# A transformer layer on one core: the output projection as seven half-size products, with its weight sums, one modulation row and several loads made elsewhere

## The chip, the core and the metric

The kernel runs on one core of one Trainium2 chip. The metric is the device time of one execution in microseconds. Three runs of the kernel before took 1303.9, 1304.48 and 1306.3 us; the median is 1304.48 us.

## The reference

One layer on 512 tokens of width 1024, in float32. Three stages each add to x, and each normalises x and modulates it with three of nine rows (`sh`, `sc`, `g`) that are computed from a conditioning vector c:

```python
mod = jax.nn.silu(c) @ w_ada + b_ada          # nine rows of 1024
u = rms_norm(x, ffn1_norm_g) * (1 + sc1) + sh1
x = x + 0.5 * g1 * swiglu(u, ffn1_w_in, ffn1_w_out)
u = rms_norm(x, mix_norm_g) * (1 + sc2) + sh2
z = u @ w_mix + b_mix      # 4 mLSTM heads, 16 forgetting-attention heads, 2 gates
merged = sigmoid(g_a) * (y_a @ w_branch_a) + sigmoid(g_b) * (y_b @ w_branch_b)
x = x + g2 * (merged @ w_out)                 # 512x1024 times 1024x1024
u = rms_norm(x, ffn2_norm_g) * (1 + sc3) + sh3
x = x + 0.5 * g3 * swiglu(u, ffn2_w_in, ffn2_w_out)
```

## The kernel before

Every large product is made of triples of TensorE matmuls (`mm3`, L139): each float32 operand is split into a high part in a reduced format (`fp32r`) and the remainder, and hi·hi, hi·lo and lo·hi are summed in one PSUM bank (lines L141 to L143). ScalarE makes the high part of a weight tile (`wh`, L116) and VectorE subtracts it from the tile that was loaded (`wl`, L118). Loads go through SyncE's queue into a ring of three buffers called `raw` (L106). A `raw` buffer is free again when its `wl` is made.

The program runs through these stages: the first FFN's input product (`ffn_in`) up to about 279 us, its output product (`pair_out`) up to about 371 us, the mix norm, the gates, mLSTM and the attention heads up to about 817 us, the two branch products with the gating ("br", to 906.5 us), the product with `w_out` (to 953 us), and the second FFN. The three FFN and branch stages fill spare time of VectorE and the queues with side work that is stepped by generators: `ada_row(v)` (L305) adds up one row v of `w_ada` in eight steps, each a 512 KB load and a multiply-add on VectorE (L320), and `ada_sum` closes the row with two matmuls (L372).

In the branch stage, the two halves of a merged tile are added on GpSimd (L1691), split by ScalarE (L1692) and VectorE (L1693). The product with `w_out` has two halves of 512 columns. `token_gemm` makes half 0 into four PSUM banks (k outer, four token blocks inner), `residual` scales each finished bank with `g` and adds it to x (L796, L798), and `x_sq` (L243) sums the squares on ScalarE. `passage` makes half 1 in the same way and starts the second FFN in it: with `xnorm` (L256) and `norm_turn` (L286) it normalises and transposes tokens 0 to 255 as soon as both halves of them are done, and tokens 256 to 511 after the last block. Between these two, `first(0, ...)` runs the first products of the second FFN on tokens 0 to 255. Inside `passage` all instructions are pinned to the order in which they are written; elsewhere a scheduler orders them, and each engine then executes its list strictly in that order. A normalisation is: `v` (L261) from the sums, eight small VectorE operations (`rsqrt`, L151), two scalings on VectorE (L267) and two on ScalarE (L268), 16 transposes (L294), and per k tile a `u_part` (L272) of two ScalarE operations and one subtraction on VectorE.

In the heads, `fox_s` leaves exp'd scores S and their row sums `sm`. `fox_p` inverts the sums (L1323), scales S in four pieces (L1326, VectorE) and transposes it (L1332).

The functions that the diff touches follow.

Of the kernel before, what the change touches and what calls it, by code (L numbers as in the profile page):

```python
# [22 lines left out]
NT = 4  # L23
# [24 lines left out]
class Layer:  # L48
    def __init__(self, tc, es, A, out, dbg=None):
# [13 lines left out]
        self.due = []  # L63
        self.posts = []
# [191 lines left out]
    def xnorm(self, hf, pool):  # L256
# [5 lines left out]
        r = self.rsqrt(v, 2, self.pin, D ** 0.5)  # L262
# [410 lines left out]
    def token_gemm(self, lhs, nk, w, half, done, tail=2, extra=None):  # L673


        nch = nk // 2
        bank = self.tbank if half == 0 else self.gbank
        ps = [bank() for _ in range(NT)]
        def step(tb, ch, wc):
            for k2 in range(2):  # L680
                k = 2 * ch + k2
                lh, ll = lhs(k)
                self.mm3(ps[tb], lh[:, tb * P:(tb + 1) * P], ll[:, tb * P:(tb + 1) * P],
                         wc[0][:, k2, :], wc[1][:, k2, :], k == 0, k == nk - 1)
        for ch in range(nch - tail):
            wc = self.w_mov(w, ch * 256, half * 512)
            for tb in range(NT):
                step(tb, ch, wc)
            if extra:
                extra()  # L690
        wcs = [self.w_mov(w, ch * 256, half * 512) for ch in range(nch - tail, nch)]
        for tb in range(NT):
            for i, wc in enumerate(wcs):
                step(tb, nch - tail + i, wc)
            done(tb, half, ps[tb])

    def passage(self, lhs, w_out, w_in, bp, G, sh):

        nc, tc = self.nc, self.tc
        pin = tc.keep_in_program_order  # L700
        done = self.residual(0.5, 5, 1, bp)
        ps = [self.gbank() for _ in range(NT)]
        def step(tb, ch, wc, k2s=(0, 1)):
            for k2 in k2s:
                k = 2 * ch + k2
                lh, ll = lhs(k)
                self.mm3(ps[tb], lh[:, tb * P:(tb + 1) * P], ll[:, tb * P:(tb + 1) * P],
                         wc[0][:, k2, :], wc[1][:, k2, :], k == 0, k == NK - 1)
# [4 lines left out]
        def apart(m):  # L713
            r = load(m)
            half = lambda n: [bp.tile([P, 4, P], F32R, name=self.nm(n), tag="yl", bufs=8) for _ in range(2)]
            hi, lo = half("fh"), half("fl")
            for i in range(2):
                pin(nc.scalar.activation(hi[i], r[:, 4 * i:4 * i + 4], AF.Copy))
            ws[m] = lambda k: (hi[k // 4][:, k % 4, :], lo[k // 4][:, k % 4, :])
            def rest():  # L720
                for i in range(2):
                    pin(nc.vector.tensor_tensor(lo[i], r[:, 4 * i:4 * i + 4], hi[i], op=SUB))
            return rest
        def whole(m):
# [5 lines left out]
                    lambda: pin(nc.vector.tensor_tensor(lo, r, hi, op=SUB)))  # L730
        wc = self.w_mov(w_out, 0, 512)
        for tb in range(NT):
            step(tb, 0, wc)
        wcs = [self.w_mov(w_out, ch * 256, 512) for ch in range(1, 4)]
        self.pin = pin
        for f in whole(0):
            f()
# [23 lines left out]
        for k in range(1, 5):  # L761
            part(0, b, k, True)
# [998 lines left out]
```

## Time and profile before

| What | Value |
|---|---|
| Runs | 1303.9, 1304.48, 1306.3 us |
| Profiled execution: span | 1304.7 us (no time besides it is listed for this execution) |
| TensorE busy | 1291.3 us, 99% |
| VectorE busy | 961.2 us, 74% |
| ScalarE busy | 632.3 us, 48% |
| GpSimd busy | 34.6 us, 3% |
| Granted TensorE clock | 9 or more tenths in all 40 slices |
| DMA | 260.48 MB, 199 GB/s of HBM traffic over the span |

The shares are averages over stages with different limits. TensorE's busy time counts a matmul from its modelled start to its modelled end, and matmuls overlap, so the cost of one matmul is read from the distance between two starts. A wait shows where that distance is larger.

### The profile page before, as it was taken

Reading aid. Unit: us, or ns where it says so; the run is one execution under the profiler, and the core shown is the slowest. Engines: PE = TensorE matmul, PEld = TensorE weight load, DVE = VectorE, ACT = ScalarE, POOL = GpSimd, SP = SyncE. Lnnn points to the kernel's source line nnn. Section 1 sums busy time; section 2 is a strip of 40 time slices with the busy share of each in tenths; the row PEclk is TensorE's granted clock in tenths of the full one; section 3 lists DMA queues with packets and bytes.
Section 4 is the critical chain, followed back from the end, with each engine's and each line's share of the span. In section 5 each row is a group of like instructions: output and inputs, shape, how many; then the busy total and the mean of one; then the engine's idle time right before and its main releaser. Section 6 shows DMA issues by size and latency. Waiting matters only on the chain.

```text
span 1304.7 us, 17739 instructions
## 1 busy us (share of the span) xinstructions
PE 1291.3 (99%) x6265; PEld 1085.2 (83%) x6265; DVE 961.2 (74%) x1740; ACT 632.3 (48%) x1040; POOL 34.6 (3%) x57
## 2 busy tenths in 40 slices
PE   8999999999999999999999999999999999999998
PEld 6788888888889888788888888888898888888887
DVE  6877777478789787999998776677566656635787
ACT  5633232355467655666574766234372223223741
POOL 1000000000010101000000000003000000000000
PEclk9999999999999999999999999999999999999999
DMA  9999978464865534545455583777539778634573
GB/s 294 276 328 303 316 266 292 139 185 155 296 187 144 173 89 130 178 133 155 138 128 149 130 151 102 230 256 242 186 114 321 257 233 278 219 97 136 167 272 143
DMA packets 245257, 260.48 MB, mean 200 GB/s; under 512 B 57312, under 2 KB 184960, under 8 KB 245168
## 3 DMA queue, kind: packets, MB, share of 16 engines
q1 hardware_dynamic: 240464, 251.41, 63.0%
q10 hardware_dynamic: 4384, 7.88, 2.0%
q8 instruction: 49, 0.80, 0.3%
q14 instruction: 40, 0.33, 0.1%
q0 software_dynamic: 320, 0.06, 0.0%
HBM read 220.43 MB, written 38.87 MB: 199 GB/s over the span
## 4 chain that ended last, share of the span: by engine, by line
PE 93%; DVE 4%; DMA 1%; ACT 1%; issue 1%; POOL 0%; ACTq 0%; DVEq 0%; POOLq 0%; SPq 0%
PE g L142 24%; PE g L141 24%; PE g L143 24%; PE t L141 4%; PE t L142 4%; PE t L143 4%; PE g L949 2%; PE t L1362 1%; PE t L1332 1%; PE t L1305 1%; PE t L949 1%; PE t L1306 1%; PE t L837 0%; DVE wl L118 0%; DMA h_d<-hn 0%
## 5 line engine op out<-in xcount | busy, mean ns | idle before, releaser
L116 ACT ACTIVATE wh<-raw 128x1024 fp32r<-128x1024 f32 (+2 forms) x246 | 248.9, 1016 | 348.8 <-PE g L142 109.9
L118 DVE TENSOR_TENSOR wl<-raw,wh 128x1024 fp32r<-128x1024 f32 (+2 forms) x246 | 288.1, 1175 | 155.0 <-ACT wh L116 131.0
L141 PE MATMUL g<-uh,wh 128*128 128x512 f32 (+1 forms) x880 | 340.9, 387 | 0.0
L143 PE MATMUL g<-uh,wl 128*128 128x512 f32 (+1 forms) x880 | 339.6, 386 | 0.0
L142 PE MATMUL g<-ul,wh 128*128 128x512 f32 (+1 forms) x880 | 339.1, 385 | 0.0
L143 PEld LDWEIGHTS g<-uh,wl 128*128 128x128 f32 x880 | 165.3, 188 | 33.6
L141 PEld LDWEIGHTS g<-uh,wh 128*128 128x128 f32 x880 | 165.4, 188 | 32.9 <-issue 0.6
L142 PEld LDWEIGHTS g<-ul,wh 128*128 128x128 f32 x880 | 165.4, 188 | 32.2
L141 PE MATMUL g<-wh,uh 128*128 128x512 f32 (+1 forms) x256 | 97.6, 381 | 0.0
L143 PE MATMUL g<-wh,ul 128*128 128x512 f32 (+1 forms) x256 | 96.6, 377 | 0.0
L142 PE MATMUL g<-wl,uh 128*128 128x512 f32 (+1 forms) x256 | 96.5, 377 | 0.0
L320 DVE SCALAR_TENSOR_TENSOR acc<-raw,ccol,acc 128x1024 f32<-128x1024 f32 (+1 forms) x56 | 56.7, 1032 | 40.1 <-DMA raw<-in_w_ada_dram 40.0
L141 PE MATMUL t<-wh,A 128*128 128x512 f32 x176 | 68.6, 390 | 0.0
L142 PE MATMUL t<-wl,A 128*128 128x512 f32 x176 | 68.6, 390 | 0.0
L143 PEld LDWEIGHTS g<-wh,ul 128*128 128x128 f32 x256 | 48.2, 188 | 8.9
L142 PEld LDWEIGHTS g<-wl,uh 128*128 128x128 f32 x256 | 48.3, 188 | 8.4
L141 PEld LDWEIGHTS g<-wh,uh 128*128 128x128 f32 x256 | 48.2, 188 | 8.2
L141 PE MATMUL g<-yh,wh 128*128 128x512 f32 x128 | 49.8, 389 | 0.0
L143 PE MATMUL g<-yh,wl 128*128 128x512 f32 x128 | 49.8, 389 | 0.0
L142 PE MATMUL g<-yl,wh 128*128 128x512 f32 x128 | 49.8, 389 | 0.0
L1316 ACT ACTIVATE S<-S,mn 128x128 f32<-128x128 f32 (+1 forms) x64 | 35.6, 557 | 26.2 <-DVE mn L1308 20.4
L460 ACT ACTIVATE A<-E 128x768 fp32r<-128x768 f32 x22 | 18.6, 846 | 52.6 <-DVE E L459 52.6
(370 smaller groups left out, 2230.3 us busy)
## 6 DMA issues: line engine op xcount, KB each, us to landing
raw<-in_ffn_w_in_dram SPq DMA_DIRECT2D x82, 512.0 KB, 4.9
raw<-in_w_ada_dram SPq DMA_DIRECT2D x48, 512.0 KB, 4.8
raw<-in_w_mix_dram SPq DMA_DIRECT2D x46, 512.0 KB, 4.3
sa<-in_ffn_w_out_dram SPq DMA_DIRECT2D x22, 512.0 KB, 5.4
sb<-in_ffn_w_out_dram SPq DMA_DIRECT2D x44, 256.0 KB, 5.7
ws<-sa SPq DMA_DIRECT2D x22, 512.0 KB, 4.8
ws<-sb SPq DMA_DIRECT2D x44, 256.0 KB, 3.8
raw<-ws SPq DMA_DIRECT2D x44, 256.0 KB, 3.6
```

What stands on the lines that cost most here:

```text
L116: nc.scalar.activation(hi, src, AF.Copy)
L118: self.last_lo = nc.vector.tensor_tensor(lo, src, hi, op=SUB)
L141: pin(mm(ps, lh, rh, start=start, stop=False))
L142: pin(mm(ps, lh, rl, start=False, stop=False))
L143: self.last_mm = pin(mm(ps, ll, rh, start=False, stop=stop))
L320: nc.vector.scalar_tensor_tensor(a, r[:, s], c, a, op0=MUL, op1=ADD)
L460: nc.scalar.activation(A1[:, 0:3, :], E[:, 0:3, :], AF.Copy)
L949: pin(nc.tensor.matmul(acc_ps[b], (wl if p == 1 else wh)[:, b % 2, s], self.ul[k] if p == 2 else self.uh[k], start=k == 0 and p == 0, stop ...
L1305: nc.tensor.matmul(ps[:, :w], q[:, s], k[:, :w], start=True, stop=False)
L1306: nc.tensor.matmul(ps[:, :w], q[:, s], kl[:, :w], start=False, stop=True)
L1316: nc.scalar.activation(S[:, ws], S[:, ws], AF.Exp, scale=-1.0, bias=m, accum_out=sm[:, qb:qb + 1])
L1332: tr = lambda b, c, qb, kb: nc.tensor.transpose(b[:, c:c + P], S[:, P_OFF[qb] + kb * P:P_OFF[qb] + (kb + 1) * P], self.ident)
```

## The change

1. **The product with `w_out`** is made by a scheme of seven products of half size (256 tokens by 512 inner by 512 columns) in place of eight. Their names are A11, A12, S2, S1, S4, S3 and A22. Each has 4 k tiles, 2 token blocks and 3 matmuls of 128x512, so there are 168 matmuls in place of 192. Partial results are kept in `p1`, `u2` and `u4` and added again; S1 and S4 go on in the same two banks (`Z`) in which S2 was summed, after a copy of each (L771) was taken.
2. **Sums and differences of operands.** `merge_pair` forms those of the merged tiles on VectorE beside the branch products, and the GpSimd addition goes to VectorE. `out_sums` forms those of the weights beside heads 10 to 16: for each of four i, two loads of 256 KB and four stores on GpSimd's queue, and four additions of 128x512 on VectorE.
3. **The scaling of S** goes to ScalarE for heads 9 to 15.
4. **Modulation row 6** is added up in the first FFN's input stage (32 steps in place of 24) and not in the branches.
5. **Loads.** x, the row `g` and the rows 6 and 7 are loaded within the branches, and the 16x16 transpose of the rows (L389) goes there too. Two of the first weight tiles of the second FFN are loaded into free buffers (`fr`, four loads of 256 KB) and not through the `raw` ring.
6. **The passage** is written anew: the token blocks of x are finished in another order, all four sums of squares of tokens 256 to 511 stand behind the first `norm_turn` (before, two of them did), and `first(0, (0, 1, 2))` is one group ahead of the second `norm_turn`.

```diff
-                ada = (s for v in (3, 4, 2) for s in self.ada_row(v, new, row, self.gbank if v == 2 else self.tbank))
+                ada = (s for v in (3, 4, 2, 6) for s in self.ada_row(v, new, row, self.tbank if v < 6 and v > 2 else self.gbank))
-                    if n * 7 % 10 < 7:
+                    if n * 3 % 4 < 3 or n > 23:
                         next(ada, None)
-        self.ada = (s for v in (6, 7) for s in self.ada_row(v, new, row, self.gbank))
+        self.ada = self.ada_row(7, new, row, self.gbank)
...
-            nc.vector.tensor_scalar(S[:, ws], S[:, ws], sm[:, qb:qb + 1], None, op0=MUL)
+            if h < 9:
+                nc.vector.tensor_scalar(S[:, ws], S[:, ws], sm[:, qb:qb + 1], None, op0=MUL)
+            else:
+                nc.scalar.activation(S[:, ws], S[:, ws], AF.Copy, scale=sm[:, qb:qb + 1])
...
+    def out_sums(self, w, ip):
+        for i in range(NK // 2):
+            with self.tc.issue_after(self.last_raw.ins):
+                for r in range(2):
+                    nc.gpsimd.dma_start(t[:, 2 * r:2 * r + 2, :], w[(2 * i + r) * P:(2 * i + r + 1) * P, :]
+                                        .rearrange("p (h n) -> p h n", h=2))
+            yield
+            with self.tc.issue_after(self.last_lo.ins):
+                V(a, b, a, op=SUB)
+                V(b, d, b, op=SUB)
+            yield
+            with self.tc.issue_after(self.last_lo.ins):
+                V(d, d, a, op=SUB)
+                V(c, c, d, op=SUB)
+            yield
+            for n, o in enumerate(self.wo):
+                nc.gpsimd.dma_start(o[:, i, :], t[:, n, :])
+            yield
...
             for m in range(NK):
                 t = self.branch(m, 1, bp, None)
+                nc.vector.tensor_tensor(self.merge_slot(m, yp), t, ta[m], op=ADD)
                 step()
-                nc.gpsimd.tensor_tensor(t, t, ta[m], op=ADD)
-                nc.scalar.activation(self.mh[m], t, AF.Copy)
-                nc.vector.tensor_tensor(self.ml[m], t, self.mh[m], op=SUB)
...
+                if m % 2:
+                    self.merge_pair(m // 2, bp)
+                if 0 < m < 5:
+                    self.x_tiles((m - 1,))
+                    self.x_load(self.x_d, (m - 1,))
...
+        def product(n, ps, tb, start=False):
+            s = slice(tb * P, (tb + 1) * P)
+            for i in range(NK // 2):
+                h, l = self.ma[n][i]
+                w = self.ops[n][i // 2]
+                self.mm3(ps[tb], h[:, s], l[:, s], w[0][:, i % 2, :], w[1][:, i % 2, :], start and i == 0, i == NK // 2 - 1, True)
...
+        product("S2", Z, 0)
+        copy(u2[0], Z[0])
+        t = into(1, 0, X[1], p1[1])
+        product("S2", Z, 1)
+        copy(u2[1], Z[1])
+        fetch("S4")
...
+        product("S1", Z, 0)
...
         b = self.norm_turn(0, xn)
+        product("A22", V4, 1)
...
+        t20 = into(2, 0, V4[0])
+        part(0, 0)
+        part(0, 1)
+        lo3()
+        into(2, 1, ts[0])
+        part(0, 2)
+        part(0, 3)
+        into(3, 1, ts[1])
+        part(0, 4)
+        self.x_sq(2, 0, t20)
+        part(0, 5)
+        self.x_sq(2, 1, ts[0])
+        t = into(3, 0, V4[1])
+        part(0, 6)
+        self.x_sq(3, 1, ts[1])
+        part(0, 7)
+        self.x_sq(3, 0, t)
         xn = self.xnorm(1, bp)
```

Three places show how the instruction lists change. In the rows, a line number is that of the kernel named, then come the operation, the tile written, the tiles read and the shape.

**VectorE, the second norm of the passage.** Before (`v` from the sums, seven small operations, then the scaling `xn`):

```order
L261 SCALAR_TENSOR_TENSOR v_9338<-ss_8913 128x2
L160 TENSOR_SCALAR rq_9340<-v_9338 128x2
L162 TENSOR_TENSOR rt_9341<-rq_9340 128x2
L163 SCALAR_TENSOR_TENSOR rd_9343<-rt_9341,v_9338 128x2
L164 TENSOR_SCALAR rd_9343<-rd_9343 128x2
L165 SCALAR_TENSOR_TENSOR rt_9341<-rd_9343 128x2
L166 SCALAR_TENSOR_TENSOR rt_9342<-rd_9343 128x2
L167 SCALAR_TENSOR_TENSOR rq_9340<-rt_9341,rq_9340 128x2
L168 SCALAR_TENSOR_TENSOR rq_9340<-rt_9342,rq_9340 128x2
L267 TENSOR_SCALAR xn_9352<-x_8901,rq_9340 128x512
L267 TENSOR_SCALAR xn_9356<-x_8903,rq_9340 128x512
```

Now:

```order
L262 SCALAR_TENSOR_TENSOR v_9470<-ss_9048 128x2
L161 TENSOR_SCALAR rq_9472<-v_9470 128x2
L163 TENSOR_TENSOR rt_9473<-rq_9472 128x2
L164 SCALAR_TENSOR_TENSOR rd_9475<-rt_9473,v_9470 128x2
L165 TENSOR_SCALAR rd_9475<-rd_9475 128x2
L166 SCALAR_TENSOR_TENSOR rt_9473<-rd_9475 128x2
L167 SCALAR_TENSOR_TENSOR rt_9474<-rd_9475 128x2
L119 TENSOR_TENSOR wl_9773<-raw_9770,wh_9772 128x1024
L168 SCALAR_TENSOR_TENSOR rq_9472<-rt_9473,rq_9472 128x2
L119 TENSOR_TENSOR wl_9820<-raw_9817,wh_9819 128x1024
L169 SCALAR_TENSOR_TENSOR rq_9472<-rt_9474,rq_9472 128x2
L272 TENSOR_SCALAR xn_9484<-x_8823,rq_9472 128x512
```

Two splits of weight tiles for the second FFN (`wl`) stand inside the chain of small operations, where before they stood behind `xn`.

**ScalarE, the beginning of the product with `w_out`.** Before (`mh` are high parts of merged tiles, `rs` the sums of squares, L729 and L718 weights of the second FFN):

```order
L116 ACTIVATE wh_8954<-raw_8952 128x1024
L1692 ACTIVATE mh_8089<-sg_8778 128x512
L116 ACTIVATE wh_8987<-raw_8985 128x1024
L1692 ACTIVATE mh_8090<-sg_8819 128x512
L116 ACTIVATE wh_8993<-raw_8991 128x1024
L1692 ACTIVATE mh_8091<-sg_8861 128x512
L116 ACTIVATE wh_9084<-raw_9082 128x1024
L116 ACTIVATE wh_9114<-raw_9112 128x1024
L243 ACTIVATE rs_9009,ss_8913<-x_8897 128x512
```

Now (`p` and `u` are copies of the banks, `fh` weights of the second FFN, `wh` the operands S2 and then S1):

```order
L771 ACTIVATE p_1762_9052<-t_9050 128x512
L771 ACTIVATE p_1763_9053<-t_9051 128x512
L799 ACTIVATE fh_9079<-fr_9075 128x512
L799 ACTIVATE fh_9080<-fr_9076 128x512
L755 ACTIVATE wh_9110<-raw_9071 128x1024
L755 ACTIVATE wh_9114<-raw_9073 128x1024
L799 ACTIVATE fh_9104<-fr_9100 128x512
L799 ACTIVATE fh_9105<-fr_9101 128x512
L755 ACTIVATE wh_9150<-raw_9130 128x1024
L755 ACTIVATE wh_9154<-raw_9132 128x1024
L244 ACTIVATE rs_9157,ss_9048<-x_8721 128x512
L771 ACTIVATE u_1764_9054<-t_9050 128x512
```

The copy `u_1764`, after which S1 may go on in its bank, stands behind the weights `fh`, four weight splits and the sum of squares `rs_9157`.

**ScalarE in the heads.** Before (`Ph` are high parts of transposed scores, `th` and `ya` belong to the mLSTM output, L1316 is the exponential):

```order
L116 ACTIVATE wh_7759<-raw_7757 128x1024
L1389 ACTIVATE th_7780<-g_7732,hom 128x512
L1330 ACTIVATE Ph_7790<-t_7792 128x512
L1330 ACTIVATE Ph_7790<-t_7799 128x512
L1330 ACTIVATE Ph_7790<-t_7806 128x256
L1391 ACTIVATE ya_7877<-ht_7763,hmg 128x512
L1316 ACTIVATE S_7826,sm_7828<-S_7826,mn_7827 128x128
L1316 ACTIVATE S_7826,sm_7828<-S_7826,mn_7827 128x256
L1316 ACTIVATE S_7826,sm_7828<-S_7826,mn_7827 128x384
L116 ACTIVATE wh_7854<-raw_7852 128x1024
```

Now, at the corresponding place:

```order
L117 ACTIVATE wh_7660<-raw_7658 128x1024
L1501 ACTIVATE yt_7697<-t_7688 64x512
L1462 ACTIVATE S_7632<-S_7632,sm_7634 128x128
L1462 ACTIVATE S_7632<-S_7632,sm_7634 128x256
L1466 ACTIVATE Ph_7720<-t_7722 128x512
L1466 ACTIVATE Ph_7720<-t_7729 128x512
L1462 ACTIVATE S_7632<-S_7632,sm_7634 128x384
L1462 ACTIVATE S_7632<-S_7632,sm_7634 128x512
L1466 ACTIVATE Ph_7720<-t_7736 128x256
L1527 ACTIVATE ya_7766<-ht_7664,hmg 128x512
L117 ACTIVATE wh_7743<-raw_7741 128x1024
```

Four scalings of S (L1462) stand between two weight splits `wh`.

## Rows read from the trace of the kernel before

**Rows 1.** The page: busy time by engine (section 1), and the chain by engine (section 4).
```profile
PE 1291.3 (99%) x6265; PEld 1085.2 (83%) x6265; DVE 961.2 (74%) x1740; ACT 632.3 (48%) x1040; POOL 34.6 (3%) x57
PE 93%; DVE 4%; DMA 1%; ACT 1%; issue 1%; POOL 0%; ACTq 0%; DVEq 0%; POOLq 0%; SPq 0%
```

**Rows 2.** Stretches: length, busy of PE, PEld, DVE, ACT, POOL, then PEclk, DMA, GB/s.
```profile
60.00:80.00 20.00, 20.00 (x90) 16.55 (x89) 17.65 (x26) 7.98 (x9) 0.00 (x0) 1.00 0.96 337
240.00:260.00 20.00, 20.00 (x90) 16.57 (x89) 8.75 (x11) 6.32 (x8) 0.00 (x0) 1.00 0.43 124
767.00:779.00 12.00, 12.00 (x64) 10.25 (x63) 9.28 (x27) 8.77 (x19) 0.00 (x0) 1.00 0.43 75
906.50:953.00 46.50, 46.50 (x214) 38.05 (x213) 26.61 (x46) 19.90 (x38) 2.31 (x2) 1.00 0.52 165
```

**Rows 3.** TensorE in time: start us, us, engine, line, operation, out<-in.
```profile
905.77 0.39 PE L141 MATMUL g<-yh,wh 128*128 128x512 f32 x1
907.13 0.39 PE L141 MATMUL t<-wh,mh 128*128 128x512 f32 x1
...
928.48 0.39 PE L143 MATMUL t<-wh,ml 128*128 128x512 f32 x1
928.80 0.23 PE L389 MATMUL t<-ident,mr 16*128 16x16 f32 x1
928.96 0.50 PE L141 MATMUL g<-wh,mh 128*128 128x512 f32 x1
929.30 0.39 PE L142 MATMUL g<-wl,mh 128*128 128x512 f32 x1
...
961.44 1.91 PE L294 MATMUL t<-ident,xn 128*128 128x128 f32 x16
```

**Rows 4.** VectorE in time, second norm of the passage.
```profile
957.38 0.15 DVE L261 SCALAR_TENSOR_TENSOR v<-ss 128x2 f32<-128x2 f32 x1
958.95 0.88 DVE L267 TENSOR_SCALAR xn<-x,rq 128x512 f32<-128x512 f32 x2
```

**Rows 5.** ScalarE in time, the same stretch.
```profile
955.37 0.63 ACT L243 ACTIVATE rs<-x 128x512 f32<-128x512 f32 x1
956.45 0.55 ACT L279 ACTIVATE uf<-t,sh,G 128x256 f32<-128x256 f32 x1
```

**Rows 6.** DMA issues, whole program: out<-in, queue, count, KB each, us to landing.
```profile
raw<-in_ffn_w_in_dram SPq DMA_DIRECT2D x82, 512.0 KB, 4.9
x<-x_d SPq DMA_DIRECT2D x16, 256.0 KB, 4.3
raw<-in_w_mix_dram SPq DMA_DIRECT2D x4, 6.0 KB, 3.3
rowsA<-in_b_mix_dram POOLq DMA_DIRECT2D x2, 4.0 KB, 5.3
```

**Rows 7.** SyncE's queue in time, one issue.
```profile
920.33 0.37 SPq L106 DMA_DIRECT2D raw<-in_ffn_w_in_dram  x1
```

**Rows 8.** Groups by line: count, busy us, mean ns, idle before.
```profile
L320 DVE SCALAR_TENSOR_TENSOR acc<-raw,ccol,acc 128x1024 f32<-128x1024 f32 (+1 forms) x56 | 56.7, 1032 | 40.1 <-DMA raw<-in_w_ada_dram 40.0
...
L1326 DVE TENSOR_SCALAR S<-S,sm 128x128 f32<-128x128 f32 (+1 forms) x64 | 21.0, 381 | 0.5
L798 DVE TENSOR_TENSOR x<-x,rs 128x512 f32<-128x512 f32 x8 | 5.5, 692 | 0.2
...
L1316 ACT ACTIVATE S<-S,mn 128x128 f32<-128x128 f32 (+1 forms) x64 | 35.6, 557 | 26.2 <-DVE mn L1308 20.4
...
L718 ACT ACTIVATE fh<-raw 128x512 fp32r<-128x512 f32 x4 | 2.3, 621 | 0.4 <-DMA raw<-in_ffn_w_in_dram 0.4
```

**Rows 9.** VectorE in time, a weight split in the heads.
```profile
769.38 1.23 DVE L118 TENSOR_TENSOR wl<-raw,wh 128x1024 fp32r<-128x1024 f32 x1 [0.70 <-ACT wh L116]
770.52 0.28 DVE L1308 CUSTOM_DVE_ANT_0 S<-t,Am 128x128 f32<-128x128 f32 x1
```

**Rows 10.** TensorE in time, the product that reads it.
```profile
771.37 0.40 PE L143 MATMUL g<-uh,wl 128*128 128x512 f32 x1
```

More of the change, by code (lines that the diff above doesn't have):

```diff
@@ L697, in passage @@
[L697 to L708 removed]
+    def out_sums(self, w, ip):
+        nc = self.nc
+        V = nc.vector.tensor_tensor
+        self.wo = [self.dp.tile([P, NK // 2, 512], F32, name=self.nm("wo")) for _ in range(4)]
+        t = ip.tile([P, 4, 512], F32, name=self.nm("so"), tag="vm", bufs=3)
+        a, b, c, d = [t[:, n, :] for n in range(4)]
+        for i in range(NK // 2):
[15 more added lines that the diff above has]
+            yield
@@ new lines, in out_src, with fetch @@
+    def out_src(self, w_out):
+        T1, T3, T4, T2 = self.wo
+        wv = w_out.rearrange("(i h p) n -> h p i n", h=2, p=P)
+        raw_w = lambda r, h: lambda c: wv[r][:, 2 * c:2 * c + 2, h * 512:(h + 1) * 512]
+        sum_w = lambda t: lambda c: t[:, 2 * c:2 * c + 2, :]
+        self.osrc = {"A11": raw_w(0, 0), "A12": raw_w(1, 0), "S4": raw_w(1, 1),
+                     "S1": sum_w(T1), "S3": sum_w(T3), "A22": sum_w(T4), "S2": sum_w(T2)}
+        self.ops, self.raws = {}, {}
+    def fetch(self, n):
+        self.raws[n] = [self.raw([P, 2, 512], [(lambda t: t, self.osrc[n](c))]) for c in range(2)]
+        self.ops[n] = []
@@ new lines, in passage @@
+        Z = [self.tbank() for _ in range(2)]
+        self.pin = pin
+        p1, u2, u4 = [keep(n) for n in ("p1", "u2", "u4")]
+        with tc.issue_after(self.last_mm.ins):
+            product("A11", Z, 0, True)
+        copy(p1[0], Z[0])
+        fetch("S2")
+        fhi1, flo1 = apart(1)
+        product("A11", Z, 1, True)
+        copy(p1[1], Z[1])
+        g = self.g5
+        fhi1()
+        flo1()
+        fhi2, flo2 = apart(2)
+        X = [self.gbank() for _ in range(2)]
+        hi("S2")
@@ new lines, in passage @@
+        lo("S2", 0)
+        hi("S2")
+        lo("S2", 1)
+        product("A12", X, 0, True)
+        fetch("S1")
+        fhi2()
+        flo2()
+        product("A12", X, 1, True)
+        hi("S1")
+        lo("S1", 0)
+        hi("S1")
+        t = into(0, 0, X[0], p1[0])
+        lo("S1", 1)
+        self.x_sq(0, 0, t)
+        product("S2", Z, 0)
[4 more added lines that the diff above has]
+        fetch("S4")
+        hi("S4")
@@ new lines, in passage @@
+        lo("S4", 0)
+        hi("S4")
+        lo("S4", 1)
+        self.x_sq(1, 0, t)
+        product("S1", Z, 0)
+        copy(u4[0], Z[0])
+        into(2, 0, u2[0])
+        into(3, 0, u2[1])
+        product("S1", Z, 1)
+        copy(u4[1], Z[1])
+        fetch("S3")
+        hi("S3")
+        lo("S3", 0)
+        hi("S3")
+        lo("S3", 1)
+        product("S4", Z, 0)
+        fetch("A22")
+        t = into(0, 1, Z[0])
+        self.x_sq(0, 1, t)
+        product("S4", Z, 1)
+        hi("A22")
@@ new lines, in passage @@
+        t = into(1, 1, Z[1])
+        lo("A22", 0)
+        self.x_sq(1, 1, t)
+        hi("A22")
+        V4 = [self.gbank() for _ in range(2)]
+        product("S3", V4, 0, True)
+        v = sp.tile([P, 2], F32, name=self.nm("v"), tag="v", bufs=2)
+        s2 = self.ss[:, 0:2, :]
+        pin(V.scalar_tensor_tensor(v, s2[:, :, 0], D * EPS, s2[:, :, 1], op0=ADD, op1=ADD))
+        r = self.rsqrt(v, 2, pin, D ** 0.5)
+        ts = [free("rs") for _ in range(2)]
+        pin(V.tensor_tensor(ts[0], V4[0], u4[0], op=ADD))
```

224 lines of the change are left out of this document (116 added, 108 removed).

## The prediction

> **What bounds the kernel now.** I read the page's busy time and chain first, then the stretches, then the engines' own rows around the places that the change touches. TensorE is busy for 1291.3 of 1304.7 us and makes up 93% of the chain that ended last [rows 1]. No other engine is above 74%. The clock column shows 1.00 in every stretch that I read [rows 2], so matmuls cost the same everywhere. Within the product with `w_out` they follow each other without a gap: between 905.77 and 907.13 us lie six starts, so one 128x512 matmul costs 1.36 / 6 = 0.227 us of the path [rows 3]. The longer durations printed there overlap. The kernel is therefore a list of matmuls with few gaps. Fewer matmuls shorten it by 0.227 us each, and every microsecond by which an operand comes too late is added back. The question is what the six parts put in front of TensorE's operands.
>
> The table of stretches tells where there is room. In the product with `w_out` (906.5 to 953 us), VectorE works 26.6 of 46.5 us and ScalarE 19.9. In the heads at 767 to 779 us, ScalarE works 8.8 and VectorE 9.3 of 12 us. In the first FFN, 90 matmuls fit into 20 us both while the DMA engines are 96% busy and when they are 43% busy [rows 2].
>
> I sum against the profiled execution's span, 1304.7 us, and then shift by -0.2 us to the median of the runs, 1304.48 us.
>
> **Term 1, the seven products: -5.4 us.** 192 matmuls become 168, and 24 x 0.227 = 5.4 us. This is on the path and certain.
>
> **Term 2, the transpose L389: -0.4 us.** From L143 at 928.48 to L142 at 929.30 us pass 0.82 us where two steps of 0.227 us would do; the transpose and the change of banks cost 0.37 us [rows 3]. It now stands among branch products, where another bank is being filled. There it may cost its own 0.23 us, so the ends are -0.4 and -0.2. The two L372 matmuls of row 6 only move to the first FFN.
>
> **Term 3, a wait before S1: +1.3 us.** I count from the end of the last branch matmul. S1 goes on in the banks of S2, so it waits for the copy `u_1764`. TensorE gets there after 6 groups of 12 matmuls (A11, A12 and S2), 72 x 0.227 = 16.3 us. The copy stands on ScalarE behind what VectorE must have done first. The ring is free again for S1's load after a gating, an addition and a weight split, at about 0.69 + 0.69 + 1.23 = 2.6 us [rows 8, 9]. The `fr` loads stand behind that load on SyncE's queue; at 0.37 us per issue [rows 7] the first is issued at about 3.3 us and lands 4.3 to 4.9 us later [rows 6]. A copy of 0.62 us [rows 8] gives 8.2 to 8.8 us. Then VectorE has four `fl`, three `wl` and three operations of `into` in its list: 4 x 0.69 + 3 x 1.23 + 3 x 0.69 = 8.5 us, or about 7.7 us since starts come some 0.08 us ahead of the end before (770.52 after 769.38 + 1.23) [rows 9]. The sum of squares (0.63 us [rows 5]) and the copy (0.62) end at 17.2 to 17.8 us, 0.9 to 1.5 us late. I take 1.3, because bank changes come on top. The ends are 0 (loads land early and the list runs ahead) and 2.3 us (no overlap of VectorE's operations). What is late next is S1's second weight tile, which stands in the same list and hides in the same wait.
>
> **Term 4, a wait at the second `norm_turn`: +2.0 us.** Before, the last sum of squares on ScalarE starts at 955.37 us, the last `u_part` operation ends at 957.00 us [rows 5], `v` starts at 957.38 us and `xn` at 958.95 us, 1.57 us later [rows 4]. Half of 0.88 us later, at 959.4 us, the first transpose could begin; TensorE comes to it at 961.44 us [rows 3]. So 2.0 us are to spare. Three things use them up. (a) 12 matmuls of A22 stand behind the first turn where 15 stood: TensorE comes 3 x 0.227 = 0.7 us sooner, at 960.8 us. (b) Two more sums of squares at 0.63 us put the end of ScalarE's list at 957.00 + 1.26 = 958.3 us. (c) Two weight splits now stand inside the chain of small operations, 2 x 1.23 = 2.5 us, less their overlap 2.3 us. The first `xn` is ready at 958.3 + 1.57 + 2.3 + 0.44 = 962.6 us, 1.8 us late; with the hand-over 2.0 us. The ends are 0.5 us (the splits' other operands make the list run ahead) and 4 us: behind the first turn VectorE also has four `into` of 1.4 us, one split and eight subtractions, and is itself nearly full there.
>
> **Term 5, heads 10 to 16: +1.1 us.** VectorE gets 16 additions x 0.69 = 11.0 us and loses 7 heads x 4 x 0.381 = 10.7 us [rows 8]: nothing. ScalarE gets the scalings, for which no row of before exists. The nearest are the exponentials on the same tiles, 0.557 us [rows 8]: 4 x 0.557 = 2.2 us per head. In the busiest stretch this fills 8.8 + 2.2 = 11.0 of 12.0 us. The path is touched where a scaling stands ahead of a weight split: such a split ends at 769.38 + 1.23 = 770.61 us and TensorE reads it at 771.37 us [rows 9, 10], 0.8 us to spare. In the new list four of the seven heads' weights stand right behind scalings. The lower end is 0, since ScalarE's idle time there exceeds 2.2 us; the upper end is 4 x (2.2 - 0.8) = 5.6 us. I take a fifth, 1.1 us, since the total still fits.
>
> **Term 6, row 6 in the first FFN: +0.3 us.** Eight steps bring 8 x 512 KB and 8 x 1.03 = 8.2 us of VectorE [rows 8] into the later part of that stage, where at 240 to 260 us the DMA engines are 43% and VectorE 44% busy [rows 2]. The cover is that idle time. Without it, one load that comes late costs half a landing of 4.9 us [rows 6]; the ends are -0.2 (the branches lose eight steps) and 2.4 us.
>
> **At nothing.** `merge_pair` on VectorE lies beside the branch products. Per step of 24 x 0.227 = 5.4 us it has a gating, an addition, a split and half a pair, 0.69 + 0.69 + 1.23 + (3 x 0.69 + 5 x 0.35) / 2 = 4.5 us, with half-size operations put at 0.35 us, half of 0.69. The ada steps that left make the room. Were it gone, the last pair would start A11 late by a copy and a subtraction, 1.3 us. The moved loads of x and rows are ten issues x 0.37 us of SyncE over 43 us; if they held up a branch weight it would be by one issue.
>
> **Sum.** -5.4 - 0.4 + 1.3 + 2.0 + 1.1 + 0.3 = -1.1 us: 1303.6 us by the profiled execution, **1303.4 us** against the median. Of a gain of 5.8 us, the list orders give most back.
>
> **Rivals.** (A) *All covered.* The waits of terms 3 to 6 stay within their slack, because VectorE is only 57% busy in that stretch today. 1304.5 - 5.8 = 1298.7 us. For it: 2.0 us of slack at the second turn. Against it: the two splits inside the chain are fixed by the order of the list.
>
> (B) *ScalarE sets the pace in the heads* (slower). The scalings in ScalarE's list delay the weight behind them in four of seven heads by all of 2.2 - 0.8 us: 5.6 us in place of 1.1, so 1303.4 + 4.5 = 1307.9 us. It decides from the point where a scaling delays `wh` by more than 0.8 us. For it: 11.0 of 12.0 us full, in strict order. Against it: the scores are ready several microseconds before their transposes, so scalings seldom wait themselves.
>
> (C) *The weight sums' loads come late* (slower). They are issued by GpSimd's queue, and VectorE's subtractions stand in its list as if they were there. A 4 KB load from this queue landed after 5.3 us where a 6 KB load from SyncE's took 3.3 us [rows 6], 2.0 us longer. If four loads are late by this, less 0.8 us of slack, the price is 4 x 1.2 = 4.8 us: 1308.2 us. Against it: several microseconds lie between load and use. The Trainium skill, page "SBUF — State Buffer", section "A bandwidth-pool intuition that's wrong (but worth ruling out)", says that a GpSimd-issued DMA of about 620 ns took some 3100 ns beside VectorE copies, as its descriptors could not be written; by that the delay would be 2.5 us and the price, as an estimate, 6.8 us. No row here shows it, for the only such loads ran at the start with VectorE nearly idle.
>
> That the change would not save 24 matmuls is excluded by the code.
>
> **Chances.** The forecast has 0.52, A 0.28, B 0.14, C 0.06. About 0.2% (2.6 us) is what a measurement can tell from no change, so faster means below 1301.9 us, slower above 1307.1 us. Faster: nine tenths of A and a tenth of the forecast, 0.25 + 0.05 = 0.30. Slower: four fifths of B and C, 0.16, and a tenth of the forecast, 0.05: 0.21, rounded up to 0.22 as the upper ends reach further than the lower. Same: 0.48. The forecast's own range is 1301 to 1307 us. The range 1299.2 to 1307.8 us leaves out the lowest third of A and about half of B and C, some 0.19.
>
> **What would show it.** Right: the `w_out` stage is 5.4 us of matmuls shorter; TensorE idles about 1.3 us before the first S1 matmul, with ScalarE's copy as releaser, and about 2 us before the second L294 group, with VectorE's or ScalarE's `xn` as releaser; heads 10 to 16 lose under 2 us. Wrong: those two waits under 0.5 us in sum (A); weight splits in the heads releasing TensorE with over 0.5 us per head (B); additions of `so` waiting for a DMA (C); or a new wait in the first FFN behind L320.

## The result and the profile after

The changed kernel takes 1311.93 us (median of four runs, 1311.31 to 1312.04) against 1305.39 us for the kernel before (median of four runs, the three given above and one of 1307.1). The ratio is 1.0046 with an interval of 1.0031 to 1.0060: slower, and outside the predicted range. The profiled execution has a span of 1310.3 us, 5.6 more than before.

Busy time and the chain of waits, from the page of the changed kernel (line numbers are its own from here on):

```profile
PE 1290.7 (99%) x6241; PEld 1081.7 (83%) x6241; DVE 981.7 (75%) x1764; ACT 657.6 (50%) x1086; POOL 34.9 (3%) x73
...
PE 72%; DMA 12%; DVE 9%; ACT 4%; issue 2%; SPq 1%; ACTq 0%; DVEq 0%
```

Twenty-four matmuls are gone, yet TensorE's busy time has hardly moved: a matmul that follows a wait, or that runs at the lower clock, has a longer record. The chain shows the loss at once. Before, TensorE made up 93% of it [rows 1]; now a DMA is in it with 12%.

To place the loss I took the distance between the starts of neighbouring matmuls less the median distance for the shape, and summed that by stretch:

| Stretch, us | Before | After | Difference |
|---|---|---|---|
| the first matmul's start | 5.97 | 4.94 | -1.0 |
| 0 to 60 | 5.8 | 7.1 | +1.3 |
| 220 to 260, first FFN | 0 | 5.1 | +5.1 |
| 520 to 560, after the mLSTM | 3.2 | 1.0 | -2.2 |
| 740 to 820, heads 10 to 16 | 0.5 | 1.9 | +1.4 |
| 820 to 920 | -0.1 | 0.2 | +0.3 |
| 920 to 980, `w_out` and the passage | 0.4 | 6.5 | +6.1 |
| 24 matmuls x 0.227 us | | | -5.4 |

These make up the 5.6 us. A sum counts waits and also matmuls that ran slowly behind them. The rows of the start swing from profile to profile: 0 to 60 us came out at 5.7 to 8.0 us in the kernels of the experiments. The two large terms are the first FFN and the product with `w_out`. The stretches of the changed kernel (columns as in [rows 2], where PEclk is the granted clock) show the first from 220 us on and the second from 906.5 us on:

```profile
220.00:240.00 20.00, 19.33 (x85) 15.68 (x85) 14.38 (x18) 5.95 (x8) 0.00 (x0) 1.00 0.75 247
240.00:260.00 20.00, 16.33 (x71) 12.72 (x71) 14.49 (x16) 5.99 (x8) 0.00 (x0) 1.00 0.71 212
767.00:779.00 12.00, 11.76 (x60) 9.71 (x59) 9.66 (x26) 8.71 (x20) 1.08 (x2) 1.00 0.60 143
906.50:953.00 46.50, 44.65 (x203) 36.24 (x202) 38.96 (x61) 27.98 (x44) 0.00 (x0) 1.00 0.62 196
```

At 240 to 260 us 71 matmuls stand where 90 stood [rows 2], with the DMA engines only 71% busy; at 60 to 80 us of the kernel before, 90 stood beside 96% [rows 2]. So bandwidth doesn't look short. In the product VectorE works 39.0 of 46.5 us; it worked 26.6 before [rows 2].

**The first FFN.** Four views of the changed kernel belong together. First the waits of all engines between 220 and 260 us (total, times, longest):

```profile
ACT wh L117 <- DMA raw<-in_ffn_w_in_dram: 32.0, 8, 7.4
DVE wl L119 <- ACT wh L117: 7.8, 4, 3.1
...
PE g L377 <- ACT sl L438: 3.2, 1, 3.2
```

Then SyncE's queue in time, its loads into the `raw` ring:

```profile
217.33 0.36 SPq L107 DMA_DIRECT2D raw<-in_w_ada_dram  x1
217.94 0.84 SPq L107 DMA_DIRECT2D raw<-in_ffn_w_in_dram  x1
221.61 0.33 SPq L107 DMA_DIRECT2D raw<-in_w_ada_dram  x1
...
227.05 0.39 SPq L107 DMA_DIRECT2D raw<-in_ffn_w_in_dram  x1
...
233.87 0.38 SPq L107 DMA_DIRECT2D raw<-in_ffn_w_in_dram  x1
```

VectorE, which uses them:

```profile
216.64 1.27 DVE L325 SCALAR_TENSOR_TENSOR acc<-raw,ccol,acc 128x1024 f32<-128x1024 f32 x1
...
229.10 1.22 DVE L372 TENSOR_TENSOR hl<-acc,hl 64x1024 fp32r<-64x1024 f32 x1
...
231.56 0.74 DVE L323 TENSOR_SCALAR acc<-raw,ccol 128x1024 f32<-128x1024 f32 x1
...
232.56 1.28 DVE L325 SCALAR_TENSOR_TENSOR acc<-raw,ccol,acc 128x1024 f32<-128x1024 f32 x1
```

And ScalarE, ahead of `sl`:

```profile
238.99 1.06 ACT L117 ACTIVATE wh<-raw 128x1024 fp32r<-128x1024 f32 x1 [7.40 <-DMA raw<-in_ffn_w_in_dram]
...
242.55 1.06 ACT L117 ACTIVATE wh<-raw 128x1024 fp32r<-128x1024 f32 x1 [1.77 <-DMA raw<-in_ffn_w_in_dram]
243.51 1.07 ACT L438 ACTIVATE sl<-g 128x512 f32<-128x512 f32 x2
```

Row 2's last multiply-add starts at 216.64 us. Its accumulator has one place, and closing the row (`ada_sum`) holds it until L372 ends at 230.3 us. The loads of row 6 don't wait for the accumulator; they only need a `raw` buffer. So two of them are issued at 217.33 and 221.61 us and lie in two of the three buffers until 231.56 and 232.56 us, 14 and 11 us. One buffer is left for the FFN's weights: their loads stand at 217.94, 227.05 and 233.87 us. ScalarE's `wh` waits 7.4 us for the last of them and the next `wh` another 1.8 us for its own load. `sl` (which frees TensorE's bank) stands behind both on ScalarE, and TensorE comes to L377 3.4 us late.

**The product and the passage.** TensorE's own rows, before S1 and before the second `norm_turn`:

```profile
928.50 0.39 PE L144 MATMUL t<-wh,mo 128*128 128x512 f32 x1
930.21 0.50 PE L142 MATMUL t<-wh,mo 128*128 128x512 f32 x1 [1.32 <-ACT u L771]
...
963.04 0.28 PE L144 MATMUL g<-uh,fl 128*128 128x256 f32 x1
965.14 3.18 PE L299 MATMUL t<-ident,xn 128*128 128x128 f32 x16 [1.82 <-DVE xn L272]
```

From start to start these are 1.71 and 2.10 us, so 1.48 and 1.98 us too much. Between them, 0.55 us are lost before A22 at 946.44 us, and two weight splits cost 0.3 us or less each. The 16 transposes take 3.18 us where 1.91 were enough before [rows 3], and the stretches behind them tell why:

```profile
966.00:967.00 1.00, 1.00 (x7) 1.00 (x6) 0.00 (x0) 0.97 (x3) 0.00 (x0) 0.55 0.72 162
967.00:968.00 1.00, 1.00 (x8) 1.00 (x6) 0.43 (x2) 1.00 (x4) 0.00 (x0) 0.50 0.88 297
968.00:969.00 1.00, 1.00 (x7) 1.00 (x6) 0.51 (x2) 1.00 (x3) 0.00 (x0) 0.50 0.29 102
969.00:970.00 1.00, 1.00 (x8) 1.00 (x8) 0.51 (x2) 1.00 (x3) 0.00 (x0) 0.74 0.00 0
```

The granted clock is at its lower level from 966 to about 969.5 us. That makes up nearly all of the 1.8 us that 960 to 980 us loses besides the wait.

### The profile page after: what moved, and what is told of

Same layout as the page of the kernel before. It is cut to its first block, busy times and chain, and to the rows that moved or that the text cites. A ratio compares the mean times of both kernels' runs of the same rounds, so it can differ in the third digit from the quotient of the medians.

```text
span 1310.3 us, 17832 instructions
## 1 busy us (share of the span) xinstructions
PE 1290.7 (99%) x6241; PEld 1081.7 (83%) x6241; DVE 981.7 (75%) x1764; ACT 657.6 (50%) x1086; POOL 34.9 (3%) x73
## 4 chain that ended last, share of the span: by engine, by line
PE 72%; DMA 12%; DVE 9%; ACT 4%; issue 2%; SPq 1%; ACTq 0%; DVEq 0%
PE g L144 18%; PE g L142 18%; PE g L143 18%; DMA raw<-in_ffn_w_in_dram 7%; PE t L142 3%; PE t L143 3%; PE t L144 3%; DMA raw<-in_w_ada_dram 2%; DVE wl L119 2%; ACT wh L117 2%; PE t L1498 1%; PE t L1468 1%; PE g L1082 1%; DVE acc L325 1%; PE t L1438 1%
## 5 line engine op out<-in xcount | busy, mean ns | idle before, releaser
L117 ACT ACTIVATE wh<-raw 128x1024 fp32r<-128x1024 f32 (+2 forms) x238 | 240.4, 1015 | 365.2 <-DMA raw<-in_ffn_w_in_dram 132.1
L119 DVE TENSOR_TENSOR wl<-raw,wh 128x1024 fp32r<-128x1024 f32 (+2 forms) x238 | 276.9, 1168 | 151.1 <-ACT wh L117 143.7
L325 DVE SCALAR_TENSOR_TENSOR acc<-raw,ccol,acc 128x1024 f32<-128x1024 f32 (+1 forms) x49 | 54.8, 1128 | 49.8 <-DMA raw<-in_w_ada_dram 49.7
L143 PE MATMUL g<-wl,A 128*128 128x512 f32 x108 | 42.4, 392 | 0.0
```

The costliest lines, as they stand in the source:

```text
L117: nc.scalar.activation(hi, src, AF.Copy)
L119: self.last_lo = nc.vector.tensor_tensor(lo, src, hi, op=SUB)
L143: pin(mm(ps, lh, rl, start=False, stop=False, skip_group_check=on))
L325: nc.vector.scalar_tensor_tensor(a, r[:, s], c, a, op0=MUL, op1=ADD)
```

## The experiments

My theory was that the loss is these two places, each a matter of who stands in front of whom, and that either can be repaired by order alone. The rivals: the first FFN lacks DMA or VectorE time for eight more steps; and the product is bound by VectorE's total work, so that a wait taken away comes back. In all, thirteen runs. "Waits" below are sums as in the table above, so they hold slow matmuls too: in the first FFN, stretches at a granted clock of 0.50 behind a wait make up about 1.6 us of the sum in after_again, 2.3 in e5, 2.4 in e6 and 1.7 in e10. The runs were made on four chips, so kernels are compared by their ratios to the kernel before.

**e1_even.** The row steps spread evenly, 16 of 19 slots.

```diff
-                    if n * 3 % 4 < 3 or n > 23:
+                    if n * 16 % 19 < 16:
```

> The same 32 steps of modulation rows in the first FFN's input stage, spread evenly over its 38 slots (16 of every 19) instead of 3 of 4 up to slot 24 and every slot from then on. Bytes, additions and their engine are unchanged. Theory R (ring): with one weight load and one row load in every slot, three buffers turn over too slowly, and TensorE waits 5.1 us between 234 and 253 us; with 1.84 loads per slot the wait there falls under 1 us and the time by 3.5 to 5 us, to about 1307.5 us. Rival D (bandwidth): the row's 4 MB are too much for the DMA engines in this stage whatever their order; the wait stays within 1 us of 5.1 us and the time is the same.

Measured: 1307.33 us, ratio 1.0020 (1.0008 to 1.0032). The wait in the first FFN is 1.8 us in this profile. By the ratios some 3.4 us are gained, but that the even rate lowered the wait is not shown: e2's profile has 1.6 us there with the steps unaltered, and e6's, with the same even steps, 7.1 us.

**e2_chain.** Two weight splits of the second FFN put behind both scalings `xn`.

```diff
+        if self.hold:
+            with self.tc.issue_after(self.last_xn[1].ins):
+                nc.scalar.activation(hi, src, AF.Copy)
+            with self.tc.issue_after(self.last_xn[0].ins):
+                self.last_lo = nc.vector.tensor_tensor(lo, src, hi, op=SUB)
...
+            self.hold = 2
```

> The two weight splits of the second FFN that stood inside the second norm's chain of small operations may start only behind the scaling xn. Theory: the 2.0 us wait before the second group of transposes goes (the two splits are 2.3 us), and with it the stretch at half the granted clock behind it, 1.8 us more: the time falls by 3.0 to 3.8 us, to about 1308.5 us. Rival: the wait is set by the four sums of squares on ScalarE, and the slow stretch by the transposes themselves: the time falls by under 1 us, and the clock column still shows 0.5 behind the transposes.

Measured: 1308.14 us, ratio 1.0015 (1.0004 to 1.0027). The wait at the second turn and the low clock behind it are gone (0.0 after 960 us); 1.0 us now stands before A22. Term 4's cause (c) is shown. The first FFN, which this edit doesn't touch, waited 1.6 us in this profile and 5.1 in the changed kernel's, so single profiles of that stage swing by some 3.5 us.

**e3_copy.** The copy of S2's bank put ahead of a sum of squares.

```diff
-        self.x_sq(0, 0, t)
         product("S2", Z, 0)
         copy(u2[0], Z[0])
+        self.x_sq(0, 0, t)
```

> In ScalarE's list, the copy of the bank that S1 goes on in stands ahead of the first sum of squares instead of behind it. Theory: the copy no longer waits for VectorE's three operations of the block (they end at 928.8 us), so the 1.48 us wait before S1 falls to 0.3 us or less and the time by 1.0 to 1.5 us. Rival: the wait is S1's second weight tile, whose load came late behind the four fr loads: the wait moves three matmul groups on and the time falls by under 0.4 us.

Measured: 1311.25 us, ratio 1.0049 (1.0032 to 1.0066). The waits of TensorE in this kernel between 915 and 980 us:

```profile
PE g L142 <- ACT xn L273: 2.1, 1, 2.1
PE t L299 <- DVE xn L272: 1.7, 1, 1.7
```

S1's wait is gone, and 2.2 us now stand at 945 us before A22: 2.7 us in both kernels for 920 to 960 us. The view names ScalarE's `xn`, but A22 goes on in a bank that this addition on VectorE frees, behind the norm's small operations:

```profile
946.97 0.69 DVE L886 TENSOR_TENSOR rs<-g,u 128x512 f32<-128x512 f32 x1
...
947.80 0.47 PE L142 MATMUL g<-wh,mr 128*128 128x512 f32 x1 [2.07 <-ACT xn L273]
```

The wait before S1 had only covered one that VectorE's list makes later. The expectation's own rival (S1's second weight tile) is not what came, but that of the section is borne out here: a wait taken away comes back.

**e4_back.** Row 6 again in the branches, closed before the products.

```diff
-        self.ada = self.ada_row(7, new, row, self.gbank)
+        self.ada = (s for v in (6, 7) for s in self.ada_row(v, new, row, self.gbank))
...
+            self.tick(8)
+            G3, sh3 = self.mod_cols(6, gain(R_N3), self.mod_load(6), self.tbank)
```

> Modulation row 6 is added up in the branch stage again, as in the kernel before, and the 16x16 transpose of the rows stands ahead of the seven products again; all else as in the changed kernel. Theory R: the first FFN's input stage loses its 5.1 us of waits, the transpose costs some 0.4 us, and VectorE, which now also forms the operands of the products beside the branches, has 1.0 us more to do in each of eight steps of 5.4 us: if that fits, the time falls by 4 to 5 us, to about 1307.5 us. Rival: the branches then lose what the first FFN gains, 2 to 5 us between 820 and 912 us, and the time is within 2 us of the changed kernel's.

Measured: 1323.11 us, ratio 1.0133 (1.0118 to 1.0148). The first FFN's wait is 0, so row 6, with the denser steps that it needs there, is what makes it. But the row then ends too late for the passage, as TensorE's rows in this kernel show:

```profile
914.68 0.59 PE L377 MATMUL g<-hl,unit 128*2 128x512 f32 x1 [0.66 <-DVE hl L372]
926.17 0.28 PE L394 MATMUL t<-ident,mr 16*128 16x16 f32 x1 [10.90 <-DMA mr<-mod_d]
```

That costs 17.4 us in four waits that begin between 897 and 915 us, far over what I had expected of it. The wait of 2 us at 529 us of the kernel before is back too.

**after_again.** The changed kernel once more, as a measure for the runs around it.

> The changed kernel once more, unaltered, since the first FFN's wait differed between profiles of kernels with the same code there (5.1, 1.6 and 6.1 us). If that wait is the sum of a loop through three buffers (ring), it swings with the landing times of the loads; the wait between 220 and 260 us lies anywhere between 1.5 and 6 us and the time between 1308 and 1312 us. Rival: it is a fixed cost of bytes; the wait is 5.1 us again within 0.5 us.

Measured: 1311.32 us, ratio 1.0045 (1.0031 to 1.0060). The first FFN's wait is 5.9 us here, not within 0.5 us of 5.1, so it is no fixed cost. From 920 to 980 us it loses 4.6 us in place of 6.5, since the stretch at the lower clock didn't come.

**e5_own.** Every second load of row 6 through a buffer of its own, in two halves.

```diff
+                    r = self.altp.tile([P, 512], F32, name=self.nm("xa"), tag="xa", bufs=1)
+                    self.last_raw = nc.sync.dma_start(r, A["w_ada"][0, k * P:(k + 1) * P, v * D + h * 512:v * D + (h + 1) * 512])
```

> From slot 24 of the first FFN on, every second row step loads its two halves through a buffer of its own (two loads of 256 KB, one behind the other), not through the ring of three; the place comes from one scratch buffer less (3 in place of 4) in that stage. Same bytes, same slots, the same additions (in halves). Ring theory: the ring then carries 1.5 loads per slot and the waits of TensorE between 220 and 260 us fall below 0.7 us; the time falls by 2 to 5 us unless the missing scratch buffer costs something in the output product. Bandwidth theory: the waits stay between 1.5 and 6 us.

Measured: 1313.02 us, ratio 1.0058 (1.0037 to 1.0078), the wait 8.7 us: missed. The second half needs the buffer of the first and waits for it on SyncE's queue, ahead of the weights' loads. The edit moved the blockade from the ring to the queue, and tells nothing against the theory or for it.

**e6_best, e7_best_dve.** e6: the edits of e1, e2 and e3, with the addition that makes `ts[0]` and both splits of A22 ahead of the first norm's small operations. e7 is e6 with the scaling of S on VectorE in all heads, as before the change.

> Four repairs together: row steps spread evenly in the first FFN; the two weight splits behind the second norm's scaling; S1's bank copy ahead of the sum of squares; and, in the first norm, the addition that frees the bank of A22 and both splits of A22 ahead of the norm's chain on VectorE instead of behind it. The copy alone gained nothing, because TensorE then waited 2.2 us before A22 for that addition (which stood behind the chain). Theory: waits at S1 and A22 together fall from 2.2 to about 1.0 us, the second turn's 3.8 us go, the first FFN's go to under 1.8 us: 1303 to 1306 us, between 6 and 9 us less than the changed kernel. Rival: VectorE bounds the whole w_out stage, so that what is moved ahead pushes the first norm back by as much, and the waits at A22 and the first turn together stay over 2 us.

> As e6_best, and the scaling of S on VectorE in all heads again. Theory B: the weight splits in heads 10 to 16 were late on ScalarE by up to 0.4 us each because scalings stood ahead of them; with ScalarE relieved the waits of 1.3 us in excess between 755 and 800 us go, and the time falls by about 1 us. Rival: VectorE, with 16 additions of 0.69 us more in these heads, becomes late itself: the waits there stay at 1.3 us or grow to 3 us.

Measured: e6 1306.97 us, ratio 1.0017 (1.0006 to 1.0029); e7 1308.05 us, 1.0022 (1.0011 to 1.0034). In e6 the waits from 920 to 980 us fall to 2.7 us, from 6.5 in the first profile of the changed kernel and 4.6 in after_again. The first FFN has 7.1 us where under 1.8 were expected. All four repairs together gain no more than e1 or e2 alone (1.0020 and 1.0015). In e7 the waits from 700 to 820 us grow from 2.2 to 3.1 us, the longest by this row of e7:

```profile
761.62 0.39 PE L1445 MATMUL t<-fk,fq 128*128 128x256 f32 x1 [0.84 <-DVE Pl L1471]
```

The intervals overlap, so by time the two are not told apart. The waits don't settle it either: after_again and e10, with the scaling on ScalarE, have 2.8 and 2.7 us in the same stretch.

**e9_pause, e10_all, e11_pause2.** Empty steps between rows, so that a row's first load comes when the accumulator is free. e9 has two before row 6 alone, on the changed kernel; e10 has that on e6; e11 has two between all rows and a step in every slot, on the passage of e6. The edit of e11:

```diff
+                def rows():
+                    for v in (3, 4, 2, 6):
+                        yield from [] if v == 3 else [None, None]
+                        yield from self.ada_row(v, new, row, self.tbank if v < 6 and v > 2 else self.gbank)
...
-                    if n * 3 % 4 < 3 or n > 23:
+                    if True:
```

> The row steps of the first FFN spread evenly as in e1_even, but two empty steps stand between the last step of row 2 and the first of row 6 (34 steps in 38 slots, 17 of every 19). Theory H (held buffers): row 6's first two loads were issued while its accumulator, which has one place, was still being folded for row 2; they lay in the ring for 14 and 11 us (issued at 217 and 222, used at 232 us) and left one buffer for the weights. With the pause the loads are used when they land: the waits of TensorE between 220 and 260 us, 1.8 to 7 us in six profiles, fall below 0.8 us, although the loads per slot rise from 1.84 to 1.89. Of the time some 2 to 4 us go against the changed kernel's 1311.5. Rival R (turnover): the ring is simply too slow for 1.9 loads per slot, and the waits stay at 1.5 us or more.

> As e6_best, with the pause of e9_pause. Theory H: of the 7 us of waits in the first FFN of e6_best's profile under 0.8 remain, and its spread of runs from 1304.2 to 1309.2 us narrows towards the lower end: 1302 to 1305 us, the same as the kernel before or faster by up to 0.2%. It stays above 1300 us if the wait for VectorE's subtraction hl near 530 us (2 us in the kernel before, gone where the first FFN was late) comes back. Rival R: 1306 to 1308 us.

> As e10_all, with two empty steps between all rows and a step in every slot (38 of 38). Theory H: only held buffers cost; with no load ever issued ahead of its accumulator, even two loads per slot turn over, and the waits in 60 to 260 us stay below 1 us. Rival R: two loads per slot are too many for three buffers; then each stretch of eight steps loses 1 us or more, 3 to 6 us in all, and it is slower than e10_all by as much.

Measured: e9 1308.91 us, ratio 1.0040 (1.0025 to 1.0055); e10 1308.69 us, 1.0035 (1.0022 to 1.0047); e11 1304.92 us, 1.0004 (0.9994 to 1.0013). e9 missed: 2.2 us remain at 220 to 240 us, and 1.8 us appear at 160 to 200 us, where the rows before change over in the same way. At 220 to 240 us it is no longer a held load; VectorE, in strict order, stands in row 6's second step until its load lands, and the operation that frees TensorE's bank (`E`) comes behind it:

```profile
225.86 1.28 DVE L325 SCALAR_TENSOR_TENSOR acc<-raw,ccol,acc 128x1024 f32<-128x1024 f32 x1 [5.02 <-DMA raw<-in_w_ada_dram]
...
230.26 0.50 PE L142 MATMUL g<-uh,wh 128*128 128x512 f32 x1 [1.92 <-DVE E L452]
```

e10 missed by more: 7.0 us from 60 to 260 us where under 0.8 were expected, and no gain over e6. e11, which pauses at every change of rows, runs the stage without a wait although it offers a step in every slot:

```profile
220.00:240.00 20.00, 20.00 (x90) 16.34 (x89) 16.26 (x20) 4.60 (x6) 0.00 (x0) 1.00 0.76 243
240.00:260.00 20.00, 20.00 (x90) 16.59 (x89) 11.35 (x14) 5.65 (x7) 0.00 (x0) 1.00 0.69 216
```

Ninety matmuls in 20 us, beside the same DMA share: DMA bandwidth and VectorE's total are refuted as causes. Between e10 and e11, on one chip, only the pauses and the step rate differ, and the rate is higher in e11; it is 3.8 us faster, with intervals that lie apart.

**e12_pause_only, e13_lo3.** e12 has the pauses of e11 alone, with the product as changed. e13 is e11 with one split (`lo3()`) moved behind the second `xnorm`.

> The change with one edit: two empty steps between the modulation rows of the first FFN and a step in every slot, so that a row's loads are issued only once the row before has given back its accumulator. Held-buffer theory: waits of TensorE over 0.15 us between 60 and 260 us under 1 us in all (5.1 in the changed kernel), and some 5 us less than it, 1306 to 1307 us; the waits after 920 us stay at 6 to 7 us, since nothing there is touched. Rival, that the loss is mainly in the product with w_out and the first FFN's wait moves elsewhere: 1309 us or more, though the FFN's wait is gone.

> As e11_pause2, with the split of S's last operand moved behind the second normalization on VectorE's list. If that split lengthens the chain before the second turn: the waits at 943 and 950 us (1.0 and 0.74 us) shrink to under 0.8 us together, and the time is 0.7 to 1.0 us below e11_pause2's, at or just below the kernel before. Rival, VectorE's total work in this stage sets it: the wait comes back at the next operand that VectorE makes, and the time stays within 0.3 us of e11_pause2's.

Measured: e12 1307.58 us, ratio 1.0011 (1.0001 to 1.0022); e13 1305.60 us, 0.9998 (0.9989 to 1.0007). e12's time is near what held buffers would give: between after_again's 1.0045 and 1.0011 lie 0.34%, or 4.4 us (the ends of the two intervals allow 1 to 8 us). Its waits were to fall under 1 us and are 3.2 from 60 to 260 us, by these rows of e12:

```profile
PE g L377 <- DVE E L452: 1.2, 1, 1.2
PE g L144 <- DVE wl L119: 0.7, 1, 0.7
PE g L142 <- DVE br L379: 0.7, 1, 0.7
```

The longest no longer begins with a load held for 11 us; as in e9, VectorE stands in a multiply-add for row 6's own load (2.65 us at 224.57 us), with `E` behind it. From 920 to 980 us e12 loses 4.6 us, as after_again does, and not the 6 to 7 expected. So e11's zero was a good draw: e13, with the same code there, waits 2.6 us. In e13's product the wait behind the split is gone and one at the second turn has come instead:

```profile
961.55 1.62 PE L306 MATMUL t<-ident,xn 128*128 128x128 f32 x11 [1.03 <-DVE xn L279]
```

From 940 to 980 us e13 loses 2.2 us and e11 1.9. The rival holds there: the wait moves with VectorE's list. No version got measurably below the kernel before; e11 and e13 can't be told from it.

## Why the prediction was wrong

**Term 6 (row 6, +0.3 us, at most 2.4) failed.** It measured +5.1 and +5.9 us in two profiles of the changed kernel (the second with about 1.6 us at the lower clock). I had costed eight loads and eight multiply-adds against idle DMA and VectorE time, and that cover was there: e11's profile has all of them without a wait. What I left out is the resource a load occupies before it is used. My price for the missing cover, half a landing of 4.9 us, was for one late load; the real chain is two buffers of three held for 11 to 14 us, weights loaded one by one, `wh`, then `sl`, then TensorE. e4 shows that row 6 is the cause, and e11 and e12 that much of it hangs on when a row's loads are issued against the closing of the row before. What e12 and e13 keep is put down by rows alone, and no run tried it: the longest wait in each to VectorE standing in row 6's own steps, and 0.7 us in each to the addition `br`, which frees the bank in which the row was closed. The prediction did name "a new wait in the first FFN behind L320" as a sign of being wrong; in the changed kernel its largest part came behind `wh` and `sl` of ScalarE. Behind that multiply-add (L325 there) it stands in e9 and e12.

**Term 4 (second turn, +2.0 us) was right in its wait**, 1.98 us with `xn` as releaser, and e2 shows the cause (c). It missed what followed in that profile, some 1.7 us at the lower clock.

**Term 3 (S1, +1.3 us)** measured 1.48 us, with the copy as releaser. The releaser and the size were right, but not what the wait is worth: with the copy early (e3) it is gone, and the same VectorE list delays A22 by as much. I had no term for A22 (+0.55 us) or for the two splits at up to 0.3 us.

**Term 5 (heads, +1.1 us)** measured +1.4, with weight splits as releasers at three places (0.41, 0.38 and 0.22 us). **Rival B** (5.6 us there) is refuted. So is **rival C**: of the rows of GpSimd's queue,

```profile
so<-in_w_out_dram POOLq DMA_DIRECT2D x8, 512.0 KB, 5.7
wo<-so POOLq DMA_DIRECT2D x16, 256.0 KB, 3.8
```

the loads landed 5.7 us after issue beside a busy VectorE, against 4.4 us for weights of that size from SyncE, and no wait of TensorE from 740 to 820 us names them. One addition of `so`, at 711 us, waited 1.4 us for its load, and TensorE lost nothing by it (0.2 us from 700 to 740 us, as before). (Each is 512 KB; the 256 KB given in the section on the change are the stores' size.) The Trainium skill, page "SBUF — State Buffer", section "A bandwidth-pool intuition that's wrong (but worth ruling out)", has such a DMA take five times as long beside a VectorE copy (620 to 3100 ns). Here 5.7 against 4.4 us is 1.3 times, so a delay of that size was not seen. **Rival A** is refuted by the waits of terms 3 and 4, 3.5 us in sum. Its argument was that VectorE is "only 57% busy in that stretch today"; with the change it is 39.0 / 46.5 = 84%.

**Terms 1 and 2** (-5.4 and -0.4 us) hold: the `w_out` matmuls that are left follow each other at 0.227 us.

**Not foreseen at all**: 2.2 us less around 530 us, where before the closing of a row on TensorE waited for `hl` (L372 and L367 of before). The wait is absent in the kernels with row 6 in the first FFN and back in e4. Why the earlier row has this effect wasn't tried and stays open. The start, code with the same instructions, came out 0.3 us longer, less than it swings between profiles.

Put together: for terms 2 to 4 I had 1.3 + 2.0 - 0.4 = 2.9 us, and the product and the passage lost 6.1, so 3.2 us are missing there. Term 6 lacks 4.8, the heads and branches 0.6, the start 0.3; 2.2 us came back at 530 us. -1.1 + 3.2 + 4.8 + 0.6 + 0.3 - 2.2 = 5.6 us, as measured. Some 1.7 of the 3.2 us are the clock's, which after_again didn't lose there.

## What to carry to other kernels

Before side work is moved beside a stream of weights, count for how long each of its loads holds a place of the shared ring: from its issue until its consumer runs, and the consumer may be waiting for an accumulator that has nothing to do with the load. Idle shares of the DMA engines and of VectorE don't show this; pauses at the change of rows gave back about 4.4 us. And where an engine goes from 57% to 84% busy in a strictly ordered list, a wait that is taken from one operand is likely to come back at the next, so the saved matmuls should be counted against that engine's work first.

## What the hardware showed unexpectedly

The granted TensorE clock fell to the lower of its two levels, 1.2 GHz, behind some waits and not behind others of the same length. In the changed kernel the wait of 1.98 us before the 16 transposes at 965 us was followed by some 3.4 us at the lower level (rows above); in after_again the same wait was 1.92 us and no such stretch came. In the first FFN it was the other way round: behind 3.4 us of waiting the changed kernel ran at 1.00, and after_again, behind as much, at this:

```profile
244.00:246.00 2.00, 2.00 (x8) 1.64 (x7) 1.58 (x2) 0.19 (x1) 0.00 (x0) 0.75 0.84 242
246.00:248.00 2.00, 2.00 (x6) 1.55 (x5) 0.84 (x1) 1.05 (x1) 0.00 (x0) 0.50 0.65 180
248.00:249.00 1.00, 1.00 (x5) 0.79 (x5) 0.00 (x0) 0.00 (x1) 0.00 (x0) 0.79 0.75 248
```

Of the twelve profiles with a wait in the first FFN, six show such a stretch behind it, with a longest wait of 2.04 to 4.68 us, and six don't, with a longest wait of 0.8 to 3.40 us. So a wait of 2 us on TensorE can cost nearly 4, and one profile doesn't tell whether it will.
